# A causal two-layer decoder on one Trainium2 core: the second weight sum of a product slab, placed directly before the slab's first piece

## The chip, the core and the metric

The kernel runs on one core of a Trainium2 chip. Five engines work side by side and wait for each other through semaphores: TensorE (PE, matrix products), VectorE (DVE, elementwise work), ScalarE (ACT, copies, casts and functions), GpSimd (POOL) and SyncE (SP, which here only issues transfers). Each engine works through its own queue in order. The metric is the time of one execution in device microseconds; lower is better. It is given as the median of several runs, and beside it stands one profiled execution, from which all durations come.

## What is computed

The reference is a decoder of two layers on 256 tokens of width 2048, in float32. What matters here is the feed-forward part that closes each layer:

```python
D_MODEL = 2048
SEQ = 256
D_FF = 4 * D_MODEL

def squared_relu_mlp(h, w1, w2):
    z = jax.nn.relu(h @ w1)
    return (z * z) @ w2

for i in range(DEPTH):          # two layers
    ...
    x = x + jnp.concatenate([token_out, mem_out], axis=-1) @ w_out[i]
    x = x + squared_relu_mlp(rms_norm(x, ffn_norm[i]), w_ff1[i], w_ff2[i])
```

`w1` is 2048 x 8192 and `w2` is 8192 x 2048. The parts ahead of it (a pooling mixer, memory attention, differential attention, and their projections) are not touched by the change.

## The kernel before

**Precision.** A float32 product is made of three matmuls. Each weight is split into a high part, which ScalarE makes by a cast (line 177), and a low part, the weight minus its high part, which VectorE makes (line 178). The activations are split in the same way. PE then adds up activation-low by weight-high, activation-high by weight-high and activation-high by weight-low. So no weight reaches PE before both ScalarE and VectorE have handled it. The split parts lie in a ring of six slots of 512 columns (`hi_ring`, `lo_ring`); a slot is free again when PE has used it.

**Two kinds of weight.** Plain weights come as transfers of 128 x 1024 (`raw`, four buffers), each used as two pieces of 512 columns ("N" in the plan). One piece feeds four blocks of a plain matrix product, whose lines are 426 and 428. The second feed-forward matrix comes for the most part as product slabs ("S"). A slab covers two rows and two columns of 128 x 512 blocks, B11 and B21 in its left half `ra`, B12 and B22 in its right half `rb`. It is multiplied by the seven-product scheme of Strassen and Winograd, in which seven products of block sums do the work of eight. Lines 850, 852 and 853 are the three matmuls of each product, and line 853 is the one that reads the low part. There are 56 slabs in each feed-forward part, 112 in all.

**The weight sums of a slab.** The seven products need sums of the four blocks:

- The first sum, B11 + B12, is made by the transfers alone: `first_sum` loads B11 into a small buffer `t1` through SyncE (line 151), and GpSimd issues a transfer that adds B12 to it (line 152). There are three such buffers.
- The second sum ("K" in the plan) is the first sum minus B22. VectorE makes it at line 199 and writes it where B12 would stand in `rb`. It needs the first sum and the transfer of B22 (line 142).
- The differences of the second sum and B11, B21 are made at line 211, in place in `ra`, after the first piece has been split.

A slab is used in four pieces, each of them one split (one cast, one low part): piece 0 is B11 and B21 (two products), piece 1 the first sum (one product), piece 2 the second sum and B22 (two), piece 3 the two differences (two). Pieces 0, 2 and 3 have 1024 columns, piece 1 has 512.

**Buffers.** The left halves, and the right halves of the slabs with even numbers, take three buffers in turn (named `slab` in the profile). The right half of a slab with an odd number goes to a spare buffer inside `room`, as do the `t1` buffers. So `room<-room` at line 199 is the second sum of an odd slab, and `slab<-room,slab` that of an even one.

**Order.** The program runs twice: once dry, to collect the order in which pieces are used, and once for real. `Plan.close` turns the used order into a list of preparations, and puts each slab's K two entries (`KOFF`) ahead of its piece 0. `Feed.fill` keeps the preparations three entries (`AHEAD`) ahead of use; a K counts as an entry. `Feed._prepare` first issues loads up to three or four transfers beyond what the entry needs (`LOADS`, `loads_ahead`), and then makes the sum or the split. The list of loads follows the list of preparations: where K stands, the two transfers of its slab are entered, and with a slab's left half the first-sum transfers of the following slab are issued.

In the feed-forward part, up to 64 tiles of the first matrix (plain pieces, `up_tile`) alternate with slab pieces by a schedule of due times (`due`, `tiles_at`), about as many plain pieces as slab pieces in the middle. After every four slabs the seven accumulators change between two column groups: `swap` copies them to and from SBUF on ScalarE (lines 917 and 909). Auxiliary work is queued some steps later through `at` and `tick`: the squared ReLU (lines 811 to 815), the split of the activations (766 and 770), their block sums (786 to 797).

The kernel is written in a framework that places all semaphores and also chooses the order of the instructions on each engine, within the dependencies, from estimated times. `Feed.order` adds an edge that fixes the order of two instructions and no more. Before, such edges exist at one place for second sums: `gate` holds the first sum made in each feed-forward part behind an addition to the residual.

Of the kernel before, what the change touches and what calls it, by code (L numbers as in the profile page):

```python
# [22 lines left out]
LAM_INIT = 0.8 - 0.6 * math.exp(-0.3)  # L23
NH = 725
NBLK = 5796
SLOTS, AHEAD, LOADS, KOFF, RAWS = 6, 3, 3, 2, 4
PER_PART = 56
CN = 0.5 ** (1.0 / 3.0)
LNC = math.log(CN)
# [26 lines left out]
class Plan:  # L56
# [13 lines left out]
    def close(self):  # L70
        prep = []
        for job in self.jobs:

            if job[0] == "S" and job[2] == 0:
                prep.insert(max(0, len(prep) - KOFF), ("K", job[1]))
            prep.append(job)
        self.prep = prep
        self.where = {job: i for i, job in enumerate(prep)}
        self.loads = []
        self.need = {}  # L80
        for p in prep:
            if p[0] == "K":
                self.loads += [("S", p[1], 0), ("S", p[1], 1)]
            elif p[0] == "N" and p[1] % 2 == 0:
                self.loads.append(("N", p[1] // 2))
            self.need[p] = len(self.loads) - 1
        rows = sorted(self.loads, key=lambda r: r[0] == "N" and 8 * r[1] + 8 > self.npos)
        self.row = {r: h for h, r in enumerate(rows)}
        of = {}
        pos = 0  # L90
        for what in self.entries:
            of.setdefault(pos // 8, []).append(what)
            pos += what[4]
        self.order = []
        for r in rows:
            self.order += of[r[1]] if r[0] == "N" else self.slabs[r[1]][r[2]]


class Feed:
# [72 lines left out]
    def _split(self, job, src, n):  # L172
        a = self._slots(n)
        if a is None:
            return False
        hi, lo = self.hi[:, a * 512 : (a + n) * 512], self.lo[:, a * 512 : (a + n) * 512]
        self.last_cast = self.nc.scalar.copy(hi, src)  # L177
        low = self.nc.vector.tensor_sub(lo, src, hi.bitcast(F32))  # L178
        if self.behind:
            self.order(low, self.behind)  # L180
            self.behind = None
        self.split[job] = (hi, lo, range(a, a + n))
        return True

    def _prepare(self, p):
        sub, add = self.nc.vector.tensor_sub, self.nc.vector.tensor_add
        self.load(self.plan.need[p] + 1 + self.loads_ahead)
        if p[0] == "N":
            r = ("N", p[1] // 2)
            c = p[1] % 2 * 512  # L190
            if not self._split(p, self.raw[r][:, c : c + 512], 1):
                return False
            if c:
                del self.raw[r]
            return True
        ra, rb = self.raw[("S", p[1], 0)], self.raw.get(("S", p[1], 1))
        t1 = self.t1[p[1] % len(self.t1)]
        if p[0] == "K":
            one = sub(rb[:, 0:512], t1, rb[:, 512:1024])
            if self.gate:  # L200

                self.order(one, self.gate)
                self.gate = None
            return True
        src, n = ((ra, 2), (t1, 1), (rb, 2), (ra, 2))[p[2]]
        if not self._split(p, src, n):
            return False
        if p[2] == 0:
            t2 = rb[:, 0:512].unsqueeze(1).to_broadcast([P, 2, 512])
            two = ra.rearrange("p (a c) -> p a c", a=2)  # L210
            sub(two, t2, two)
        if p[2] == 1:
            self.t1_of[p[1] % len(self.t1)] = None
        if p[2] == 3:
            del self.raw[("S", p[1], 0)], self.raw[("S", p[1], 1)]
        return True
# [68 lines left out]
def program(ctx, tc, plan, dry, xT, memT, par, lam, cst, wst, yT):  # L285
# [972 lines left out]
    def out_tiles(l, cat, lead, ks, fx, between, later):  # L1258
# [24 lines left out]
        for n in range(NK):  # L1283
            if n < len(first):
                ps = first[n]
                a_part(ps, "w_out", l, n, ks, cat, first=False)
            else:
                ps = tile_bank(n)
                a_part(ps, "w_out", l, n, every + ks, cat)
            if n < len(later) and later[n]:  # L1290
                at(later[n], lambda ps=ps, n=n: close(ps, n))
            else:
                close(ps, n)
# [343 lines left out]
```

## Time and profile before

| | before |
|---|---|
| median of 3 runs | 2026.28 us |
| lowest and highest run | 2023.08 and 2027.01 us |
| profiled execution | 2023.32 us |
| its span, first to last instruction | 2021.6 us |
| mean granted TensorE clock | 1.000 |

The profile's page gives the busy time of each engine, and groups of instructions by source line, engine and operation, with the names of the tiles written and read (`lo_ring<-slab,hi_ring`). The table of waits names, for each group, what ended its idle time, with the total, the number and the longest wait. The timeline lists instructions with start and duration in microseconds; a bracket at the end holds the idle time just before an instruction and what ended it. SPq and POOLq rows are transfers as they are issued. Consecutive VectorE instructions overlap a little in the records, so the time that one takes in the queue is read from start to start. The two feed-forward parts lie at about 250 to 930 us and 1340 to 2020 us of the span; a stretch of both looks like this (window from 300 to 930 us and from 1365 to 2000 us; busy time of PE, PE weight loads, VectorE, ScalarE and GpSimd, then the clock, the share of the DMA engines and GB/s):

```profile
300.00:930.00 630.00, 623.90 (x3228) 529.05 (x3227) 579.64 (x895) 495.62 (x845) 43.99 (x51) 1.00 0.71 218
1365.00:2000.00 635.00, 628.32 (x3244) 532.33 (x3243) 579.25 (x889) 495.91 (x841) 44.87 (x52) 1.00 0.72 218
```

### The profile page before, as it was taken

The page shows a single profiled execution, that of the slowest core. Times are in us where ns is not written, and L with a number is a line of the kernel's source. Part 1 is how long each engine was busy: PE and PEld are TensorE (multiplying, and loading weights), DVE is VectorE, ACT ScalarE, POOL GpSimd, SP SyncE. Part 2 cuts the span into 40 slices and gives each one's busy share as a digit, 9 for nine tenths or more (in the row PEclk, how much of TensorE's full clock was granted, in tenths as well). Part 3 has the DMA queues.
Part 4 walks back from the last instruction along what each step waited for, and adds up shares of the span by engine and source line. Part 5 has one row for each costly group of instructions (what it writes and reads, how often), then busy time and mean ns, then how long its engine had stood idle before and what let it go on. Part 6 is the DMA issues. An engine that isn't in the chain of part 4 may idle for free.

```text
span 2021.6 us, 31855 instructions
## 1 busy us (share of the span) xinstructions
PE 1999.2 (99%) x10534; PEld 1702.0 (84%) x10534; DVE 1756.0 (87%) x3089; ACT 1495.9 (74%) x2791; POOL 149.9 (7%) x179
## 2 busy tenths in 40 slices
PE   9999999999999999999999999999999999999999
PEld 8888888888888888888888888888888888887888
DVE  8888878989889899999765798878989899998987
ACT  7765567787887878778665699567787878788775
POOL 0001210000000000000000000320000000000000
PEclk9999999999999999999999999999999999999999
DMA  8555577767777777755576534567767777777774
GB/s 318 170 192 188 189 204 219 228 214 234 225 209 239 218 230 213 218 183 187 187 232 193 171 123 148 190 200 218 232 196 235 225 224 224 226 225 211 224 218 134
DMA packets 142725, 420.09 MB, mean 208 GB/s; under 512 B 16096, under 2 KB 18784, under 8 KB 142560
## 3 DMA queue, kind: packets, MB, share of 16 engines
q1 hardware_dynamic: 126288, 388.69, 57.4%
q0 software_dynamic: 16128, 29.37, 8.9%
q8 instruction: 82, 1.34, 0.3%
q14 instruction: 83, 0.68, 0.1%
q10 hardware_dynamic: 144, 0.01, 0.0%
HBM read 415.90 MB, written 2.10 MB: 207 GB/s over the span
## 4 chain that ended last, share of the span: by engine, by line
PE 91%; DVE 3%; DMA 3%; ACT 2%; issue 1%; DVEq 0%; ACTq 0%
PE x_bank L426 22%; PE x_bank L428 11%; PE p L853 8%; PE p L850 8%; PE p L852 8%; PE wo L426 6%; PE wo L428 3%; DMA room<-in_w 3%; PE u L426 2%; DVE lo_ring L178 2%; PE u L428 1%; PE q L460 1%; PE q L462 1%; PE k L460 1%; PE q L461 1%; PE v L462 1%
## 5 line engine op out<-in xcount | busy, mean ns | idle before, releaser
L177 ACT CAST hi_ring<-raw 128x512 fp32r<-128x512 f32 x1001 | 609.8, 620 | 261.9 <-PE x_bank L426 60.2
L178 DVE TENSOR_TENSOR lo_ring<-raw,hi_ring 128x512 fp32r<-128x512 f32 x1001 | 681.6, 693 | 107.9 <-ACT hi_ring L177 96.2
L426 PE MATMUL x_bank<-fx,hi_ring 128*128 128x512 f32 x1920 | 600.7, 394 | 0.0
L428 PEld LDWEIGHTS x_bank<-fx,lo_ring 128*128 128x128 f32 x1920 | 360.3, 188 | 83.8 <-DVE lo_ring L178 1.6
L177 ACT CAST hi_ring<-slab 128x1024 fp32r<-128x1024 f32 x280 | 293.9, 1051 | 130.9 <-PE x_bank L426 73.5
L178 DVE TENSOR_TENSOR lo_ring<-slab,hi_ring 128x1024 fp32r<-128x1024 f32 x280 | 340.9, 1220 | 51.5 <-ACT hi_ring L177 48.9
L428 PE MATMUL x_bank<-fx,lo_ring 128*128 128x256 f32 x1920 | 377.6, 278 | 0.4 <-DVE lo_ring L178 0.4
L426 PEld LDWEIGHTS x_bank<-fx,hi_ring 128*128 128x128 f32 x1920 | 313.8, 189 | 22.7
L853 PE MATMUL p<-lo_ring,sit 128*128 128x512 f32 x448 | 175.6, 393 | 12.1 <-DVE lo_ring L178 11.9
L152 POOL DMA_DIRECT2D room<-in_w x112 | 96.9, 868 | 1144.9 <-DMA room<-in_w 1128.3
L850 PE MATMUL p<-hi_ring,sit 128*128 128x512 f32 x448 | 176.9, 395 | 2.5 <-ACT room L754 2.5
L852 PE MATMUL p<-hi_ring,sit 128*128 128x512 f32 x448 | 175.3, 391 | 0.0
L426 PE MATMUL wo<-cat,hi_ring 128*128 128x512 f32 x512 | 161.8, 397 | 0.3 <-DVE rc L397 0.3
L177 ACT CAST hi_ring<-room 128x512 fp32r<-128x512 f32 x168 | 128.4, 764 | 33.4 <-PE x_bank L426 21.7
L178 DVE TENSOR_TENSOR lo_ring<-room,hi_ring 128x512 fp32r<-128x512 f32 x168 | 144.6, 861 | 9.0 <-ACT hi_ring L177 8.9
L850 PE MATMUL p<-hi_ring,z 128*128 128x512 f32 x336 | 131.4, 391 | 1.1 <-ACT hi_ring L177 1.1
L853 PE MATMUL p<-lo_ring,z 128*128 128x512 f32 x336 | 131.3, 391 | 0.8 <-DVE lo_ring L178 0.8
L852 PE MATMUL p<-hi_ring,z 128*128 128x512 f32 x336 | 131.2, 391 | 0.0
L853 PEld LDWEIGHTS p<-lo_ring,sit 128*128 128x128 f32 x448 | 84.0, 188 | 36.5 <-DVE lo_ring L178 18.5
L428 PEld LDWEIGHTS wo<-cat,lo_ring 128*128 128x128 f32 x512 | 95.9, 188 | 22.0
L428 PE MATMUL wo<-cat,lo_ring 128*128 128x256 f32 x512 | 101.5, 279 | 0.0
L850 PEld LDWEIGHTS p<-hi_ring,sit 128*128 128x128 f32 x448 | 83.9, 187 | 12.9 <-ACT room L754 3.3
(374 smaller groups left out, 3372.4 us busy)
## 6 DMA issues: line engine op xcount, KB each, us to landing
raw<-in_w SPq DMA_DIRECT2D x500, 512.0 KB, 4.3
slab<-in_w SPq DMA_DIRECT2D x112, 512.0 KB, 4.2
room<-in_w SPq DMA_DIRECT2D x168, 256.0 KB, 3.4
room<-in_w POOLq DMA_DIRECT2D x112, 256.0 KB, 5.5
slab<-in_w SPq DMA_DIRECT2D x56, 256.0 KB, 4.3
memraw<-in_mem SPq DMA_DIRECT2D x5, 512.0 KB, 4.4
resid<-in_x SPq DMA_DIRECT2D x8, 256.0 KB, 5.6
out_y<-resid SPq DMA_DIRECT2D x16, 128.0 KB, 1.9
```

The lines of the kernel that those rows point to most:

```text
L152: self.nc.gpsimd.dma_start(self.t1[i], right, accum_op=ALU.add)
L177: self.last_cast = self.nc.scalar.copy(hi, src)
L178: low = self.nc.vector.tensor_sub(lo, src, hi.bitcast(F32))
L426: nc.tensor.matmul(ps, hi, xs[:, k, :], start=first and c == 0, stop=False)
L428: nc.tensor.matmul(ps[:, T : 2 * T], lo, xs[:, k, 0:T], start=False, stop=last and c == len(ks) - 1,)
L460: nc.tensor.matmul(ps[t], x[t][1], hi, start=k == 0, stop=False)
L461: nc.tensor.matmul(ps[t], x[t][0], hi, start=False, stop=False)
L462: nc.tensor.matmul(ps[t], x[t][0], lo, start=False, stop=k == NK - 1)
L850: nc.tensor.matmul(ps, a[1], hi, start=new, stop=False, **again)
L852: nc.tensor.matmul(ps, a[0], hi, start=False, stop=False, **again)
L853: nc.tensor.matmul(ps, a[0], lo, start=False, stop=end, **again)
```

## The change

K is entered in the list of preparations directly before piece 0 of its slab instead of two entries earlier, and `KOFF` goes. The low part of each slab piece is remembered (`last_low`), and the second sum of every slab but the first of each feed-forward part (`PER_PART` is 56) is ordered behind the low part of the slab piece that was prepared last, which is piece 3 of the preceding slab. Nothing else is edited. The lists that are derived from the preparations (places, loads, needs) follow the new order.

```diff
-SLOTS, AHEAD, LOADS, KOFF, RAWS = 6, 3, 3, 2, 4
+SLOTS, AHEAD, LOADS, RAWS = 6, 3, 3, 4
...
             if job[0] == "S" and job[2] == 0:
-                prep.insert(max(0, len(prep) - KOFF), ("K", job[1]))
+                prep.append(("K", job[1]))
             prep.append(job)
...
         low = self.nc.vector.tensor_sub(lo, src, hi.bitcast(F32))
+        if job[0] == "S":
+            self.last_low = low
         if self.behind:
...
         if p[0] == "K":
             one = sub(rb[:, 0:512], t1, rb[:, 512:1024])
+            if p[1] % PER_PART:
+                self.order(one, self.last_low.ins.name)
             if self.gate:
```

## The prediction

> **What bounds the kernel now.** I read the page's busy shares first, then the waits of TensorE (PE) and VectorE (DVE), then one stall in the timelines.
>
> ```profile
> span 2021.6 us, 31855 instructions
> PE 1999.2 (99%) x10534; PEld 1702.0 (84%) x10534; DVE 1756.0 (87%) x3089; ACT 1495.9 (74%) x2791; POOL 149.9 (7%) x179
> ```
>
> PE is busy for all but 2021.6 - 1999.2 = 22.4 us. A change that leaves the matmuls alone, as this one does, can win that much and no more. So the question is where PE waits. The waits of PE by stretch of the span, first over the two dense stretches of the feed-forward parts (300 to 930 and 1365 to 2000 us), then over the two places where such a part opens (250 to 300 and 1340 to 1365 us):
>
> ```profile
> PE p L853 <- DVE lo_ring L178: 5.8, 5, 1.7
> PE x_bank L428 <- DVE lo_ring L178: 0.2, 1, 0.2
> ...
> PE p L853 <- DVE lo_ring L178: 6.4, 5, 2.1
> PE x_bank L428 <- DVE lo_ring L178: 0.2, 1, 0.2
> ...
> PE p L850 <- ACT hi_ring L177: 1.1, 1, 1.1
> PE p L853 <- DVE lo_ring L178: 0.5, 1, 0.5
> PE p L850 <- ACT room L754: 0.2, 1, 0.2
> ...
> PE p L850 <- ACT room L754: 2.3, 1, 2.3
> ```
>
> Columns: total us, times, longest. In the dense stretches PE waits for one thing, a low part (line 178) that DVE has not finished: 5.8 + 0.2 + 6.4 + 0.2 = 12.6 us in 12 waits. The two openings cost 1.8 and 2.3 us. Now DVE's own waits at the second sum (line 199), over the whole span, and who waits for the load of line 142:
>
> ```profile
> DVE room L199 <- DMA room<-in_w: 25.9, 19, 2.9
> DVE slab L199 <- DMA room<-in_w: 11.9, 2, 6.1
> DVE slab L199 <- DMA slab<-in_w: 4.6, 6, 1.4
> ...
>   DVE room L199: 25.9, 19
>   DVE slab L199: 4.6, 6
> ```
>
> DVE stands still for 25.9 + 11.9 + 4.6 = 42.4 us in front of second sums. The first and third row are waits for the load of line 142 (the last two rows say so): the sum runs before the right half of its own slab has landed. The 25.9 us belong to odd slabs, whose sum goes to the spare buffer ("room"). One of these stalls, slabs 27 to 29, on DVE, SyncE, ScalarE (ACT) and PE:
>
> ```profile
> 591.22 1.22 DVE L178 TENSOR_TENSOR lo_ring<-room,hi_ring 128x1024 fp32r<-128x1024 f32 x1
> 592.36 0.68 DVE L199 TENSOR_TENSOR slab<-room,slab 128x512 f32<-128x512 f32 x1
> 592.96 0.28 DVE L786 TENSOR_TENSOR room<-stage 128x128 f32<-128x128 f32 x1
> 594.92 0.69 DVE L178 TENSOR_TENSOR lo_ring<-raw,hi_ring 128x512 fp32r<-128x512 f32 x1
> 597.36 0.69 DVE L199 TENSOR_TENSOR room<-room 128x512 f32<-128x512 f32 x1 [1.75 <-DMA room<-in_w]
> 597.97 2.35 DVE L178 TENSOR_TENSOR lo_ring<-slab,hi_ring 128x1024 fp32r<-128x1024 f32 x2
> ...
> 592.47 0.33 SPq L142 DMA_DIRECT2D room<-in_w  x1
> ...
> 594.78 1.06 ACT L177 CAST hi_ring<-slab 128x1024 fp32r<-128x1024 f32 x1
> 595.73 0.60 ACT L909 COPY p<-keep 128x512 f32<-128x512 f32 x1
> ...
> 599.24 0.50 PE L853 MATMUL p<-lo_ring,sit 128*128 128x512 f32 x1 [1.15 <-DVE lo_ring L178]
> ```
>
> The load of slab 29's right half goes out at 592.47, as soon as the third low part of slab 27 (591.22) frees the spare buffer. Slab 29's sum stands in DVE's queue ten microseconds too early: behind it, at 597.97, wait the last low part of slab 27 and the first of slab 28. The former had its high part by 594.78 + 1.06 = 595.84. PE stops 1.15 us for it. So a sum nobody needs for another slab (slab 29's pieces come after 608 us, below) holds up a low part that PE needs now.
>
> **The change, part by part.** The number of instructions, their shapes, matmuls and transfers stay: 112 sums, 112 loads on each of lines 138, 142, 151 and 152. What changes is the place of the sums and of what hangs on the plan.
>
> (1) *The hold.* The sum of slab n may no longer stand in front of the last low part of slab n-1. In the stall above slab 28's sum (592.36) and slab 29's (597.36) both leave the space before that low part. A sum costs DVE 592.96 - 592.36 = 0.60 us. The stall and both sums gone give 1.75 + 0.60 + 0.60 = 2.95 us against a PE wait of 1.15, bounded by the cast that ends at 595.84, 2.13 us before 597.97. So this PE wait goes with 2.13 - 1.15 = 1.0 us to spare, and slab 28's sum, now behind the low part, takes 0.60 of it. The load issued at 592.47 has then some 15 us until slab 29's sum behind slab 28's last low part (608.02 below), where the longest load in the row of (3) takes 8.8. The 12 dense waits all name the same releaser, so I take them for the same pattern, and all 12.6 us out. Bounds: 0 (another wait takes each place) and 12.6.
>
> (2) *The openings.* Slab 0 and slab 56 have no hold; their sums move behind two plain pieces in the plan. Row:
>
> ```profile
> 264.73 0.69 DVE L199 TENSOR_TENSOR slab<-room,slab 128x512 f32<-128x512 f32 x1 [6.12 <-DMA room<-in_w]
> ...
> 276.19 1.22 DVE L178 TENSOR_TENSOR lo_ring<-slab,hi_ring 128x1024 fp32r<-128x1024 f32 x1 [1.42 <-ACT hi_ring L177]
> ...
> 267.75 0.57 DVE room L199
> 268.35 1.28 DVE lo_ring L178 x2
> ```
>
> The first two rows are DVE's timeline (the second is slab 0's first low part), the others the chain that ended last. The 6.12 us wait is for the first sum's accumulating DMA, which the move does not hasten. Slab 1's sum (267.75) stands on the chain, and the hold takes it off, 0.57 us at each opening: 1.1 us. Bounds: below, 0; above, the openings' waits, 1.8 + 2.3 = 4.1 us, if slab 0's sum also lets two low parts pass. I take 1.1, because DVE fetched slab 1's sum forward past all of slab 0's pieces (267.75 against 276.19), and slab 0's sum, with no hold, can be fetched forward again.
>
> (3) *What the sums cost in the new place.* Each now stands between the last low part of one slab and the first of the next. For odd slabs that is new work there. Slab 28 to 29 (DVE, then ACT, then PE):
>
> ```profile
> 608.02 1.22 DVE L178 TENSOR_TENSOR lo_ring<-slab,hi_ring 128x1024 fp32r<-128x1024 f32 x1 [0.50 <-ACT hi_ring L177]
> 609.39 1.22 DVE L178 TENSOR_TENSOR lo_ring<-slab,hi_ring 128x1024 fp32r<-128x1024 f32 x1
> 610.54 0.69 DVE L178 TENSOR_TENSOR lo_ring<-raw,hi_ring 128x512 fp32r<-128x512 f32 x1
> ...
> 608.31 1.05 ACT L177 CAST hi_ring<-slab 128x1024 fp32r<-128x1024 f32 x1 [0.32 <-PE p L852]
> ...
> 611.54 0.39 PE L853 MATMUL p<-lo_ring,z 128*128 128x512 f32 x1
> ...
> DMA to landing us min/median/max: 2.5/4.0/8.8
> ```
>
> The low part at 608.02 occupies the queue for 610.54 - 609.39 = 1.15 us; a sum from 609.17 to 609.77 moves the next from 609.39 to 609.77, by 0.38 us. PE uses it at 611.54, 0.93 us after its end at 610.61. So here the cover is PE's preceding matmuls, and 0.55 us of it is left; without cover it would cost 0.38. Queued behind the sum are this low part, the plain one at 610.54 and slab 29's differences (line 211); PE waits for the first two. Bounds over the 54 held odd slabs: 0, and 54 x 0.38 = 20.5 us if no cover were left anywhere. The value is near the lower end, since in the dense stretches PE now waits at 12 places only; I take 1.4 us, four such shifts uncovered.
>
> (4) *Plan and loads.* The plan looks three entries ahead and counts a sum as an entry, so with the sum directly in front of the first piece, one real piece less is made ahead during the two pieces before it, and one more during the two before those. In the list of loads a slab's two transfers (with the first-sum pair behind them on SyncE and POOL) move behind a plain load that used to follow them. On SyncE most loads wait for a buffer, not for their turn, as 592.47 shows, and the order there already departs from the list (line 142 of slab 29 goes before its line 138). I set this at 0, between a gain of the 1.1 us that PE waits for a cast at an opening and the price of the slower rival.
>
> A rule bears on what is at stake. The Trainium skill ("Perfetto Trace Analysis", Identifying the Most-Contended Engine) says that matmul busy time is no measure of TensorE's headroom, that LDWEIGHTS busy is a better one, and that for VectorE occupancy is fair. By it PE has headroom (84% here), and VectorE would be what to relieve. The trace speaks against it here, since PE's few waits are single and named.
>
> **Sum.** 12.6 + 1.1 - 1.4 = 12.3 us less. The profiled execution took 2023.32 us (1.7 around its span), so 2011.0. The runs shown lie from 2023.08 to 2027.01 with the median 2.96 above the profiled one; the new median may stand 0 to 3 above its own sum, and I put it 1 above: 2012.
>
> **The rivals.**
>
> *Half is won.* Around the stall shown ACT also copies accumulators between slab groups (595.73); where such copies make a cast late, it holds the low part next. Against it: the cast was ready at 595.84 against 597.97. Half of 12.6 stays: 2012 + 6.3 = 2018.
>
> *No change.* The order of DVE is made from estimates; other work fetched forward into the space where the sums stood (the pieces of lines 786 to 797, z's low parts) keeps the low parts late. For it: 87% busy on DVE leaves little room. Against: those have no stall for a DMA in them. 2026.
>
> *Slower.* A slab's loads, now behind a plain load on SyncE, wait for that load's buffer and land late; the cast of the slab's first piece stalls and, behind it on ACT, all casts. Rows, SyncE near slab 29:
>
> ```profile
> 599.21 0.33 SPq L138 DMA_DIRECT2D slab<-in_w  x1
> 602.42 0.33 SPq L134 DMA_DIRECT2D raw<-in_w  x1
> ...
> L138 SPq DMA_DIRECT2D slab<-in_w x112: 327/328/328, 81.9 to 1970.9; - x112
> ...
> DMA to landing us min/median/max: 3.1/4.2/6.8
> ```
>
> Behind the plain load at 602.42, slab 29's left half would go at 602.75 and land at 606.95 by the median, 609.55 by the maximum, against a cast at 608.31: up to 1.2 us late. It decides once it exceeds 12.3 us, 0.23 for each of 54 odd slabs; at 1.2 us in every third (18) it is 21.6: 2012 + 21.6 = 2034. For it: the loads' list does change. Against: the order on SyncE follows the buffers.
>
> *DVE is the bound.* If DVE's stalls counted in full, 42.4 - 11.9 = 30.5 us would go: 2026.3 - 30.5 = 1996. Against it: PE cannot win more than its 22.4. The rule above would have it so.
>
> **How the numbers follow.** Forecast 0.58, half 0.11, DVE the bound 0.01, no change 0.11, slower 0.19. A difference of 0.2% (4 us) is about what a measurement of this kernel tells from none. Faster 0.58 + 0.11 + 0.01 = 0.70, same 0.11, slower 0.19. The forecast's own range is 2006 to 2016: all opening waits gone and no new cost (12.6 + 4.1 gives 2006.6 for the profiled execution) at one end, four microseconds of uncovered shifts at the other. The range up to 2027 takes in the half and the unchanged case, and leaves out the slower one.
>
> **What would show it.** Right: second sums without waits for the line 142 load (25.9 and 4.6 us gone), each between two slabs' low parts; the waits of line 853 for low parts near 1 us in place of 12.2 in the dense stretches; PE busy time as before. The 6.1 us waits at the two openings stay. Wrong: waits of casts for slab loads, of line 853 at first pieces of odd slabs, or equal PE waits with another DVE instruction in front. A sum still run before the preceding slab's last low part would mean that the hold does nothing.

## The result and the profile after

| | before | after |
|---|---|---|
| median | 2026.64 us (4 runs, 2023.08 to 2027.04) | 2008.33 us (4 runs, 2007.60 to 2009.22) |
| profiled execution | 2023.32 us | 2008.68 us |
| its span | 2021.6 us | 2006.9 us |
| TensorE busy, rest of the span | 1999.2, 22.4 us | 1996.4, 10.5 us |

The changed kernel takes 0.9914 of the time (95% interval 0.9897 to 0.9931), 18 us less by the medians and 14.6 us less by the two profiled executions. The mean granted clock of TensorE was 1.000 in both profiled executions and in all four runs after; for the other runs before it is not on record, and the last section comes back to it. In the changed file the second sum is line 201, the differences line 215, the plain product lines 430 and 432, and a slab's products lines 854, 856 and 857.

The page, the waits of PE over the whole span, and the waits of VectorE for transfers:

```profile
span 2006.9 us, 31853 instructions
PE 1996.4 (99%) x10534; PEld 1701.9 (85%) x10534; DVE 1756.0 (87%) x3089; ACT 1500.1 (75%) x2791; POOL 149.9 (7%) x179
...
PE p L854 <- ACT room L758: 1.8, 2, 1.6
PE x_bank L430 <- ACT hi_ring L177: 1.2, 2, 0.6
PE p L854 <- ACT hi_ring L177: 1.0, 3, 0.5
PE p L857 <- DVE lo_ring L178: 0.5, 1, 0.5
...
DVE slab L201 <- DMA room<-in_w: 12.2, 2, 6.3
DVE mems L1133 <- DMA memraw<-in_mem: 3.8, 1, 3.8
```

Of the 12 waits of PE for low parts in the dense stretches none is left. The 0.5 us wait at line 857 is the one at the first opening, which was there before. Of VectorE's waits in front of second sums only the two at the openings are left, 12.2 us together, and both are for the accumulating transfer of the first slab of a part. New are two waits of 0.6 us in the plain product and two of 0.2 us at line 854, all for casts.

The same place as before, slabs 27 to 29, on VectorE and then SyncE:

```profile
591.45 1.23 DVE L178 TENSOR_TENSOR lo_ring<-slab,hi_ring 128x1024 fp32r<-128x1024 f32 x1 [0.26 <-ACT hi_ring L177]
592.59 0.68 DVE L201 TENSOR_TENSOR slab<-room,slab 128x512 f32<-128x512 f32 x1
593.19 1.22 DVE L178 TENSOR_TENSOR lo_ring<-slab,hi_ring 128x1024 fp32r<-128x1024 f32 x1
...
602.31 1.22 DVE L178 TENSOR_TENSOR lo_ring<-slab,hi_ring 128x1024 fp32r<-128x1024 f32 x1 [0.23 <-ACT hi_ring L177]
603.45 0.68 DVE L201 TENSOR_TENSOR room<-room 128x512 f32<-128x512 f32 x1
604.05 1.22 DVE L178 TENSOR_TENSOR lo_ring<-slab,hi_ring 128x1024 fp32r<-128x1024 f32 x1
...
588.42 0.33 SPq L142 DMA_DIRECT2D room<-in_w  x1
```

The last low part of slab 27 (591.45) waits for its cast alone, and slab 28's sum follows it. Slab 29's right half still goes out when slab 27 lets go of the spare buffer (588.42), but its sum now stands 15 us later (603.45), and does not wait. The whole trace has this order: before, all 110 sums that can be held ran ahead of the preceding slab's last low part, 52 of them ahead of even its first; after, none does, and none stands behind its own slab's first low part.

### The profile page after: what moved, and what is told of

The parts are those of the page before. It is cut to its first block, busy times and chain, and to the rows that moved or that the text cites. A ratio compares the mean times of both kernels' runs of the same rounds, so it can differ in the third digit from the quotient of the medians.

```text
span 2006.9 us, 31853 instructions
## 1 busy us (share of the span) xinstructions
PE 1996.4 (99%) x10534; PEld 1701.9 (85%) x10534; DVE 1756.0 (87%) x3089; ACT 1500.1 (75%) x2791; POOL 149.9 (7%) x179
## 4 chain that ended last, share of the span: by engine, by line
PE 96%; ACT 1%; DVE 1%; DMA 1%; issue 0%; SPq 0%; DVEq 0%; ACTq 0%
PE x_bank L430 24%; PE x_bank L432 12%; PE p L854 9%; PE p L857 9%; PE p L856 9%; PE wo L430 6%; PE wo L432 3%; PE u L430 2%; PE ff L430 1%; PE u L432 1%; PE q L464 1%; PE k L464 1%; PE q L466 1%; PE q L465 1%; PE k L466 1%; PE v L464 1%
```

## The experiments

Theory A: what costs is a sum that VectorE's order fetches forward until it waits for its own slab's load, with the low parts behind it; the hold prevents that. Rival B: the new place in the plan, with its list of loads, does it. Within A two variants: the wait for the load costs (A1), or the mere place in the queue ahead of a low part that PE needs (A2). The kernel before, run again beside the experiments, had medians of 2027.5, 2028.0 and 2028.5 us in the three groups (e1 to e4, e5 to e8, e9 and e10); ratios are to these. The same kernel thus differs by 1 us between groups, and so much between versions of different groups is not told from none.

**e1: the place in the plan without the hold.**

```diff
             one = sub(rb[:, 0:512], t1, rb[:, 512:1024])
-            if p[1] % PER_PART:
-                self.order(one, self.last_low.ins.name)
```

> The changed kernel without the hold: the second sum stands directly before its slab in the plan, but no edge ties it to the preceding slab's last low part. Theory A (the hold is what counts, since DVE's order fetches an untied sum forward into the preceding slab): as before, 2022 to 2028 us, with 20 us or more of DVE waits for the load of line 142 in front of second sums and 8 us or more of PE waits for low parts in the product matmuls. Rival B (the new place in the plan and in the list of loads is what counts): 2007 to 2012 us and no such waits.

2030.76 us (2020.72 to 2036.19, 10 runs), ratio 1.0009 (0.9991 to 1.0028): not told from the kernel before, and above the 2022 to 2028 us expected. The waits, in a profiled execution that is the fastest of the ten:

```profile
PE p L855 <- DVE lo_ring L178: 11.1, 12, 1.6
...
DVE room L201 <- DMA room<-in_w: 20.5, 18, 2.9
DVE slab L201 <- DMA room<-in_w: 9.9, 2, 5.8
```

102 sums still ran ahead of the preceding slab's last low part. Without the hold the place in the plan does nothing: B falls.

**e2: the hold without the place.** The plan keeps its two entries, the edge is added.

```diff
-SLOTS, AHEAD, LOADS, RAWS = 6, 3, 3, 4
+SLOTS, AHEAD, LOADS, KOFF, RAWS = 6, 3, 3, 2, 4
...
-                prep.append(("K", job[1]))
+                prep.insert(max(0, len(prep) - KOFF), ("K", job[1]))
```

> The kernel before with the hold alone: the second sum keeps its place two entries ahead in the plan, and is tied behind the low part of the slab piece prepared last, which for most slabs is the third or second piece of the preceding slab, not its last. Theory A1 (what costs is the wait for the slab's own load, which is over if the sum stays out of the slab before the preceding one): 2007 to 2012 us, no waits for the load of line 142, PE waits for low parts under 3 us. Theory A2 (what costs is any sum standing in front of the preceding slab's last low part, 0.6 us each): 2013 to 2020 us, PE waits for low parts of 4 to 9 us without a load wait behind them. Rival B (the new place in the plan): 2022 to 2028 us.

2006.22 us (2005.69 to 2007.72), ratio 0.9895 (0.9870 to 0.9921), just under A1's range and 2.1 us under the changed kernel (1.0 us by the spans of the profiled executions, 2005.9 and 2006.9). 84 sums ran ahead of the preceding slab's last low part, none ahead of its first. PE's waits for products, and who waits at second sums (a part of the view of line 201):

```profile
PE p L854 <- ACT room L758: 1.8, 2, 1.6
PE p L854 <- ACT hi_ring L177: 1.5, 3, 0.5
...
PE p L857 <- DVE lo_ring L178: 0.5, 1, 0.5
...
  DMA room<-in_w: 12.4, 2
```

So a sum ahead of the last low part costs nothing that shows as long as it does not wait. That speaks for A1 and against A2, and says that a bound that keeps the sum from being fetched forward by a whole slab is enough here.

**e4: no wait, no hold.** The kernel before; an odd slab's second sum reads the first sum where it read B22.

```diff
-            one = sub(rb[:, 0:512], t1, rb[:, 512:1024])
+            one = sub(rb[:, 0:512], t1, rb[:, 512:1024] if p[1] % 2 == 0 else t1)
```

> The kernel before, but the second sum of an odd slab takes the first sum in place of the block B22, so that it does not read what line 142 loads (the block's part of the sum is left out). Sums are fetched forward as before. Theory A1 (the wait for the load costs): the 25.9 us of DVE waits go and with them most of the PE waits for low parts, 2009 to 2014 us. Theory A2 (the place in the queue costs, with or without a wait): PE waits for low parts stay at 6 us or more, 2017 to 2025 us.

2008.68 us (2006.59 to 2010.10), ratio 0.9905 (0.9879 to 0.9932). All 110 sums still ran ahead of the preceding slab's last low part, 52 of them ahead of its first:

```profile
PE p L853 <- DVE lo_ring L178: 0.5, 1, 0.5
...
DVE slab L199 <- DMA room<-in_w: 11.7, 2, 5.9
DVE slab L199 <- DMA slab<-in_w: 2.9, 5, 1.1
DVE room L199 <- DMA room<-in_w: 1.2, 2, 0.6
```

This is the cleanest of the tests: the sums in their old place, only the load taken out of the inputs of the odd ones, and the time is that of the changed kernel, just under A1's 2009 to 2014 us. A2's 2017 to 2025 us did not come, and the only wait of PE for a low part is the 0.5 us one at the first opening. The wait for the load is the cost. Against e2, which has the same plan, e4 is 2.5 us longer by the medians, but 0.6 by the spans of the profiled executions (2006.5 and 2005.9); two of its four runs had a lower granted clock (last section).

**e7 and e8: the hold on half of the slabs.** The changed kernel with the hold on odd slabs alone (e7), or on even slabs alone (e8).

```diff
-            if p[1] % PER_PART:
+            if p[1] % PER_PART and p[1] % 2:
```

In e8 the last condition is `p[1] % 2 == 0`.

> The changed kernel with the hold on the sums of odd slabs alone, whose waits for the load of line 142 were 25.9 us of the 30.5 in the kernel before. If a sum's wait is paid slab by slab, nearly all is won: 2007 to 2013 us, with DVE waits of the even slabs (the 4.6 us row) left and PE waits for low parts under 3 us. Rival: even slabs' sums, now free, are fetched forward in the place of the odd ones and wait as much: 2018 to 2030 us.

> The changed kernel with the hold on the sums of even slabs alone. If the waits of the odd slabs' sums are what is paid, as before: 2020 to 2032 us, with 18 us or more of DVE waits for the load of line 142 and 7 us or more of PE waits for low parts. Rival (two sums in a row in front of one low part are needed for a loss, and the even one is now out of the way): 2008 to 2016 us in spite of the DVE waits.

e7: 2006.98 us (2005.78 to 2007.07), ratio 0.9890 (0.9875 to 0.9905), with PE waits for low parts of 0.5 us. e8: 2033.59 us (2028.91 to 2042.84, 10 runs), ratio 1.0032 (1.0017 to 1.0046), above the 2020 to 2032 us expected. VectorE's waits in front of second sums in e7 (the openings alone), then PE's and VectorE's waits in e8:

```profile
DVE slab L201 <- DMA room<-in_w: 11.8, 2, 5.9
...
PE p L857 <- DVE lo_ring L178: 14.9, 13, 3.2
...
DVE room L201 <- DMA room<-in_w: 31.2, 20, 3.7
```

The hold on the odd slabs is the whole gain. In e7 44 sums ran ahead of the last low part, and even those waited for no load: the e7 expectation of left-over waits of even slabs did not come true. Their right half lies in the rotating buffers and is loaded earlier relative to its sum: in the kernel before, the median time from the issue at line 142 to the sum was 6.7 us for even slabs and 4.4 for odd ones, and in e7 it was 7.7 for the even ones. The odd half can only be loaded once slab n-2 has let go of the one spare buffer. In e8 the odd sums waited longer than before (31.2 against 25.9 us) and the kernel is slower than before.

**e3 and e5: the openings.** The two 6 us waits left over. In e3 the first sum of each part, too, gets an edge, behind the low part prepared last. e5 is the same with the plan of e2.

```diff
         low = self.nc.vector.tensor_sub(lo, src, hi.bitcast(F32))
+        self.last_any = low
         if job[0] == "S":
             self.last_low = low
...
             if p[1] % PER_PART:
                 self.order(one, self.last_low.ins.name)
+            else:
+                self.order(one, self.last_any.ins.name)
```

> The changed kernel, in which the second sum of slab 0 and slab 56 is also tied, behind the low part prepared last (that of the plain piece in front of it). If the 6 us waits of DVE for the accumulating transfer at the two openings are what PE pays for there (0.5 + 0.5 + 0.2 + 1.6 us idle, and about 0.3 us for each restart), those DVE waits go and the time falls by 2.5 to 4.5 us below the changed kernel, to 2004 to 2006 us. Rival: PE waits there for ScalarE's copies, which come late for another reason; then the DVE waits go and the time stays at 2007 to 2009 us.

> Plan as before (two entries ahead), sums held as in e2, and the first sum of each feed-forward part held as in e3. If the two holds act at different places (dense stretches, openings), their gains add: e2 (2006.2) less what e3 won over the changed kernel (4.6) gives 2001.6, range 2000 to 2003. Rival: they share a cause, then 2003.5 to 2006.

e3: 2003.74 us (2003.70 to 2003.98), ratio 0.9882 (0.9852 to 0.9913), 4.6 us under the changed kernel; just above the 2.5 to 4.5 that the theory gave. No wait of VectorE for a transfer in front of a second sum is left, and none of PE at the openings. e5: 2002.21 us (2002.14 to 2002.36), ratio 0.9868 (0.9852 to 0.9884), the fastest version here; the two gains add, nearly (4.0 us under e2, where 4.6 was expected). The first opening in e5, on VectorE:

```profile
257.70 0.42 DVE L818 TENSOR_TENSOR room<-room 128x256 f32<-128x256 f32 x1
259.24 0.42 DVE L329 SCALAR_TENSOR_TENSOR rs_t<-st_x,rs_t 128x256 f32<-128x256 f32 x1 [1.13 <-ACT rs_t L386]
...
264.37 0.69 DVE L202 TENSOR_TENSOR slab<-room,slab 128x512 f32<-128x512 f32 x1 [0.26 <-DMA room<-in_w]
```

The transfer lands at about the same time as before (the sum runs at 264.37, before at 264.73), but the normalisation (259.24) and four plain low parts pass in front of the sum.

**e6: the old list of loads under the new sums.**

```diff
+        old = []
+        for job in self.jobs:
+            if job[0] == "S" and job[2] == 0:
+                old.insert(max(0, len(old) - 2), ("K", job[1]))
+            old.append(job)
-        for p in prep:
+        for p in old:
             if p[0] == "K":
...
+        top = 0
+        for p in prep:
+            top = self.need[p] = max(top, self.need[p])
```

> The changed kernel with the list of loads and the needs of the kernel before: the sums stand and are held as in the changed kernel, the transfers are issued in the old sequence. Part (4) of the prediction set this at 0. If the list of loads matters little, 2006 to 2010 us with PE waits as in the changed kernel. Rival: the 2.1 us by which the changed kernel stands above e2 come from the loads; then 2005 to 2007 us and the two PE waits of 0.6 us for casts in the plain product vanish.

2008.07 us (2008.00 to 2008.22), ratio 0.9897 (0.9882 to 0.9912), as the changed kernel, and with both 0.6 us waits. The list of loads costs nothing measurable, and does not explain the 2.1 us to e2.

**e9: the run-ahead counted in real pieces** (on e3).

```diff
-        while self.pp < min(i + 1 + AHEAD, len(self.plan.prep)):
+        prep, end, n = self.plan.prep, i + 1, 0
+        while end < len(prep) and n < AHEAD:
+            n += prep[end][0] != "K"
+            end += 1
+        while self.pp < end:
```

> e3 (changed kernel with the openings held too, 2003.7), with the run-ahead counted in real pieces: a second sum no longer uses up one of the three entries. Part (4) of the prediction set the lost entry at 0. If it is what leaves a cast of a plain piece behind ScalarE's eight copies at the exchange of accumulators (PE waits of 0.6 us in the plain product, at 683.6 and 1757.8 us of the changed kernel), those two waits go and the time falls to 2001.5 to 2003.2 us. Rival: the order on ScalarE is set by readiness, not by the plan's window; then 2003.3 to 2004.5 us with both waits left.

2003.45 us (2003.39 to 2003.53), ratio 0.9879 (0.9864 to 0.9894). The time lies in the rival's range, but the waits are not the rival's: the two of 0.6 us are gone, so the lost entry did cause them. PE's waits for casts of slab pieces grew from 0.5 (e3) to 1.0 us instead, and the 0.3 us between the medians is less than two groups tell apart. In the changed kernel the place is this exchange of accumulators (the end of a run of copies on ScalarE, then PE):

```profile
681.52 0.64 ACT L913 COPY p<-keep 128x512 f32<-128x512 f32 x1
682.04 0.64 ACT L913 COPY p<-room 128x512 f32<-128x512 f32 x1
682.56 0.47 ACT L819 ACTIVATE stage<-room 128x256 f32<-128x256 f32 x1
682.88 0.65 ACT L177 CAST hi_ring<-raw 128x512 fp32r<-128x512 f32 x1
...
683.58 0.73 PE L430 MATMUL x_bank<-fx,hi_ring 128*128 128x512 f32 x2 [0.62 <-ACT hi_ring L177]
```

and in e9 the wait that took its place:

```profile
PE p L861 <- ACT hi_ring L177: 1.0, 2, 0.5
```

e2 and e5, which keep the old plan, have the same two waits of 0.5 us at these exchanges. As these rows read, ScalarE's run of copies is the limit there, and the run-ahead decides only which cast stands behind it; no run shortened the copies.

**e10: the sum behind its own slab's first piece** (the edge at the first piece's low part, and the openings included).

```diff
             if job[0] == "S" and job[2] == 0:
+                prep.append(job)
                 prep.append(("K", job[1]))
+                continue
             prep.append(job)
...
-            if p[0] == "K":
+            if p[0] == "S" and p[2] == 0:
                 self.loads += [("S", p[1], 0), ("S", p[1], 1)]
...
-            if p[1] % PER_PART:
+            if True:
                 self.order(one, self.last_low.ins.name)
...
+            t2 = rb[:, 0:512].unsqueeze(1).to_broadcast([P, 2, 512])
+            two = ra.rearrange("p (a c) -> p a c", a=2)
+            sub(two, t2, two)
             return True
...
-        if p[2] == 0:
+        if p[2] == 4:
```

So the slab's loads are entered with its first piece, and the differences are made right behind the sum; the old place of the differences is never reached.

> The changed kernel with every second sum (those of the openings too) held behind the low part of its own slab's first piece instead of in front of it. Part (3) of the prediction put 1.4 us on a sum standing in front of the first piece. To be compared with e3 (2003.7), which holds the openings too. If the place in front costs, 2002 to 2003 us; if it costs nothing, 2003.3 to 2004.5 us. Rival: the differences, which need the sum, now come late and hold up the last piece; 2005 to 2015 us with PE waits for casts of slab pieces.

2004.68 us (2003.96 to 2004.82), ratio 0.9884 (0.9867 to 0.9900), just above the 2003.3 to 2004.5 us expected for no cost, and 0.9 us above e3, where the sum stands in front. So no cost of a sum in front of the first piece shows, and the rival's waits of PE for casts of slab pieces are not there either.

## Why the prediction held, and where its sizes were off

The direction and the mechanism were right. By its own steps:

1. *The hold, 12.6 us.* The step was right: the 12 waits went, the stalls with them, and e1, e4 and e8 tie them to the wait for the odd slabs' load. What the step mis-stated is how much of the room it needs: it counted 1.75 + 0.60 + 0.60 us, stall and two sums. e4 has the two sums still in place and the gain of the stall, so the 0.60 us of a sum does not show in PE's waits, and the hold need not be behind the last low part. The last sign of being wrong (a sum still ahead of that low part means that the hold does nothing) was too strict: e2 has 84 such sums and the whole gain.
2. *The openings, 1.1 us.* PE's waits there went from 1.8 + 2.3 to 1.2 + 1.6 us, 1.3 us less; in each the longest wait is 0.6 us shorter (1.1 to 0.5 and, by the timeline, 2.25 to 1.64), as the step's 0.57 for slab 1's sum would have it. That slab 0's sum would be fetched forward again was right; e3 shows that the rest, which the prediction left unclaimed, was to be had with one more edge.
3. *The sum in front of the first piece, 1.4 us of cost.* PE waited for no low part in the dense stretches, and e10 is no faster: 0 was the value. The upper bound was slightly low, for 56 odd slabs are held and 54 even ones: 56 x 0.38 = 21.3 us.
4. *Plan and loads, 0.* For the loads right (e6). For the run-ahead wrong in place: it made the two 0.6 us waits for casts (e9), and two of 0.2 us are also new, 1.7 us of waits in all. By chance this is about the size that step 3 had booked elsewhere. They are not the net price of the new place: with the old one 1.0 us of waits stands at the same exchanges (e2, e5). By the medians of different groups the new place costs 1.5 to 2.1 us (e3 against e5, the changed kernel against e2). So the hold earns the gain, and moving K in the plan earns nothing and may give a little back; how much, and by what beyond these waits, stays open.

In idle time of PE the sum was then almost exact, with luck in its last two terms: 12.6 - 1.7 + 1.3 = 12.2 us of waits at the lines of the dense work (16.8 to 4.6). PE's whole idle time fell by 22.4 - 10.5 = 11.9 us, a little less, because a wait of 0.6 us in the memory attention (line 457) is new. But the span fell by 14.7, because PE's *busy* time fell as well, by 1999.2 - 1996.4 = 2.8 us, without one matmul less. The prediction had held that PE's busy time stays, and that the 22.4 us of idle time are all that can be won. That is the term that was mis-sized: a wait was priced at its idle time. The matmuls around the wait in the kernel before that the prediction showed at 599.24 tell why:

```profile
597.46 0.40 PE L850 MATMUL p<-hi_ring,sit 128*128 128x512 f32 x1
597.69 0.40 PE L852 MATMUL p<-hi_ring,sit 128*128 128x512 f32 x1
...
599.58 0.40 PE L850 MATMUL p<-hi_ring,z 128*128 128x512 f32 x1
```

Matmuls follow each other every 0.23 us, though each is recorded as 0.40. The one at 599.24 was due at 597.92, so it came 1.32 us late, and the next came 0.34 instead of 0.23 us after it: 1.43 us lost, where the wait is listed with 1.15. The difference of 0.28 us is hidden in records that overlap otherwise. Read in this way, the 13 waits of over 0.3 us in front of a slab's products in the kernel before give 0.26 to 0.28 us each, but for one with 0.15. There were 16 waits of PE at lines of the dense work before and 8 after, and 8 x 0.28 = 2.2 us, an estimate, is most of the 2.8. e5, with 2 such waits, has 1993.9 us of busy time.

The remaining 1.3 us between forecast and median (2012 against 2008.33, less 2.4 from the span) is the allowance for the median over the profiled execution: it was put at 1 above, and is 0.35 below. The kernel before has its median 3.3 us above its profiled execution; the granted clock is the likely reason (last section), and the prediction did not look at it.

Of the rivals, *half is won* has a true core in the exchange of accumulators, worth 1.2 us of waits and not 6. *No change* fell with the result. *Slower* by late loads: no cast waited for a slab's load, and e6 shows no effect of the list. (Casts waited 5.9 us for plain loads, 3.7 before; e2, with the old list, has 6.1.) *VectorE is the bound* would have made the span fall by the 30.5 us of stalls that went; 14.7 is what PE's waits, with the time behind each, allow. The Trainium skill's rule ("Perfetto Trace Analysis", Identifying the Most-Contended Engine) that matmul busy time does not tell TensorE's headroom has this much for it here: 99% busy hid 2.8 us that could be won.

## What to carry to other kernels

An operation without urgency that waits for a transfer can cost more than one that is late, when it stands in the in-order queue of an engine that feeds the bottleneck; look in the table of waits for DMA waits of such an engine, even if its share of busy time looks comfortable, and tie the operation behind work that is sure to come after the landing. An edge that only fixes the order did that here at no cost that shows; moving the operation in the program without it did nothing, for the framework's order still fetched 102 of 110 sums forward. In a kernel like this one, price a wait of TensorE at its idle time and about 0.3 us more, count the waits, and compare the granted clock of the runs before reading a difference of medians.

## What the runs showed that was not expected

The kernels whose VectorE waits for loads in the dense stretches do not only take longer, they also scatter more. The kernel before lay between 2021.54 and 2034.41 us in 13 runs of the first group, e1 between 2020.72 and 2036.19, e8 between 2028.91 and 2042.84. Each of the other versions lay within 3.5 us.

That the landing times of the transfers make the scatter would fit this and was not tested by itself. What goes along with it on record is the granted clock of TensorE. In its 33 executions beside the experiments the kernel before had a mean clock of 0.996 to 1.000, with a median of 0.997 in each of the three groups; the eight executions at 0.996 took 2030.0 us on average, the six at 0.999 2024.5 us. e1 and e8 also had 0.996 to 1.000. The other versions had 1.000 in every execution, but for two of e4's four (0.999 and 0.998), and these were its longest. A clock of 0.997 is worth 0.003 x 2027 = 6 us, an estimate. The profiled execution before had 1.000, so the 14.7 us of span hold nothing of this; the 19 to 26 us between the medians of the kernel before and of the versions with the gain hold some, and the 18 us of the result probably do.

Among the kept traces, e8's alone shows the clock falling before the last 2 us of the span, at two places. The first, a row of PE's timeline and then stretches of 1 us (columns as in the dense stretches before, the clock third from the end):

```profile
1364.14 0.50 PE L854 MATMUL p<-hi_ring,sit 128*128 128x512 f32 x1 [2.08 <-ACT room L758]
...
1364.00:1365.00 1.00, 0.86 (x4) 0.73 (x5) 1.00 (x4) 0.61 (x2) 0.00 (x0) 1.00 1.05 270
1365.00:1366.00 1.00, 1.00 (x6) 0.92 (x5) 0.87 (x2) 0.70 (x2) 0.00 (x0) 0.70 0.97 389
1366.00:1367.00 1.00, 1.00 (x5) 0.80 (x4) 0.31 (x1) 0.97 (x2) 0.43 (x1) 0.50 1.03 270
1367.00:1368.00 1.00, 1.00 (x5) 0.80 (x4) 1.00 (x2) 0.41 (x1) 0.43 (x1) 0.50 0.66 238
1368.00:1369.00 1.00, 1.00 (x5) 0.90 (x4) 0.93 (x4) 0.00 (x0) 0.00 (x0) 0.60 0.94 172
1369.00:1370.00 1.00, 1.00 (x8) 0.86 (x8) 0.10 (x1) 0.76 (x1) 0.00 (x0) 1.00 0.95 172
```

The clock was halved for 3.4 us, which loses 0.30 + 0.50 + 0.50 + 0.40 = 1.7 us, and it began about 1.2 us after the end of a wait of PE of 2.08 us. The second place, at 1863.74, follows a wait of 2.16 us for a low part and loses as much. A long wait is not enough: one of 3.19 us in the same trace (at 516.93) and two of 2.25 and 2.09 us in the kernel before were not followed by any. But in the traces of the versions with the gain no wait of PE is longer than 1.7 us. So the load waits probably cost some clock as well, on top of their idle time; the traces of the executions at 0.996 to 0.998 other than e8's are not kept, so this is not shown.

The right-half load of 256 KB (line 142) took 2.5 us at best, 4.0 by the median and 8.8 at worst before, and 2.5, 4.2 and 8.9 after: the hold did not make transfers faster, it only keeps VectorE from standing in front of them.
